# The last quarter of an output, added and stored in two halves of rows

## The chip, the cores and the metric

One core of one Trainium2 chip. The metric is device time in microseconds (us) of the whole program, as a median of runs; the profile's span is some 1.8 us shorter than the time of the same run.

## The reference

```
h   = x @ w1                     # x: 8 x 1024 x 1024, w1: 1024 x 4096
h   = 0.5 * h * (1 + tanh(sqrt(2 / pi) * (h + 0.044715 * h ** 3)))
out = (h @ w2).astype(float32)   # w2: 4096 x 1024, out: 8 x 1024 x 1024 in float32
```

## The kernel before

Both products are made with Strassen-like schemes on blocks; a second level of the scheme ("inner") makes each block product of the second matmul out of seven smaller ones. For the last block of 1024 rows, the last of the seven outer products (number 3) yields four quarters of a 512x512 block of the output. Each quarter is 256 rows by 256 columns: one PSUM bank of 128 partitions with two halves `i` of 256 columns each, where half `i` holds 128 rows of the output.

```python
    def store_quarter(sb, o, b, src):              # one quarter: 2 x 128 rows x 256 columns, 256 KB
        ...
        rows = out2[r0:r0 + HT // 2, o0:o0 + OH // 2].rearrange("(i p) n -> p i n", p=P)
        return nc.sync.dma_start(out=rows, in_=src)

        def multiply(self, j, bank, first):        # 16 matmuls: eight into each half of the bank
            t = self.x[S_TERM[j]] if j in S_TERM else self.s[j]
            for i in range(2):
                for c in range(NI // 2):
                    ...matmul(bank[:, i * OH // 2:(i + 1) * OH // 2], lhsT=t[:, c, i * P:(i + 1) * P], ...)

        def steps(self, into):
            a, b, c = psum(), psum(), psum()
            for n, (j, bank, first, out, adds) in enumerate((
                (1, a, True, "11", ()),
                ...                                # 2, 6, 5, 7
                (3, b, True, None, ("12",)),
                (4, a, False, "21", ()),           # the last step: adds onto bank a, gives quarter 21
            ), 1):
                self.multiply(j, bank, first)
                if out is not None:
                    t = quarter(into, out)
                    ...
                        tt(t, quarter(self.base, out), pair(bank), ADD, True)    # one VectorE add, 128x512
                ...
                        self.part(o, quarter(into, o))                           # the store of a quarter
                yield n

        # in matmul2, for the last block of rows:
        products[7].rows = out("22", accum_op=ADD)     # two 512 KB stores that add into the output
        if end:
            products[3].part = lambda b, t: store_quarter(sb, "12", b, t)
```

All semaphores and waits are placed by the program builder from the order of these calls. Transfers over SyncE's queue and over GpSimd's queue each use eight semaphores in rotation.

## Time and profile before

| | kernel before |
|---|---|
| time, median of the first three runs | 1487.91 us (1487.71 to 1488.25) |
| span of the profiled run | 1486.0 us |
| last matmul ends at | 1482.15 us |
| last add | 1482.26 to 1482.95 us |
| last store issued, landed | 1482.98, 1485.10 us |

The page and the timeline are shown in the prediction. One more view answers to a view of the changed kernel later: who SyncE waited for in the last four microseconds (engine and line, what it waited for: total us, times, longest).

```profile
SPq L1064 <- DMA out_dram<-u: 1.3, 2, 0.9
```

Line 1064 is the close of the program. Two of its waits lasted: one until the third quarter's store had landed, and one of 0.9 us until the last had. A wait that finds its store landed takes a few hundredths of a microsecond and is not in this list.

### The profile page before, as it was taken

To read this page: it belongs to the slowest core of one execution; us is meant where nothing else is said; L and a number is where in the kernel's file an instruction comes from. 1 tells how busy PE (TensorE), PEld (TensorE's weight loads), DVE (VectorE), ACT (ScalarE), POOL (GpSimd) and SP (SyncE) were. 2 spreads that over 40 slices of the span, in tenths; PEclk is the share of its full clock that TensorE was granted. 3 is DMA by queue.
4 is the path that set the end of the run, shared out by engine and by line. 5 is a ranking of instruction groups with operands and counts; after the bars stand their busy time and mean duration, and the time that the engine had idled before them with its cause. 6 is when DMAs were issued, how large, how long until landed. Compare 5 with 4: busy or idle time off the path is not lost.

```text
span 1486.0 us, 26324 instructions
## 1 busy us (share of the span) xinstructions
PE 1477.3 (99%) x9879; PEld 964.2 (65%) x9879; DVE 1149.5 (77%) x1792; ACT 613.3 (41%) x1154; POOL 231.8 (16%) x311
## 2 busy tenths in 40 slices
PE   9999999999999999999999999999999999999998
PEld 5444444444455787558875588655886568855687
DVE  6657458767677898779987799877997779877887
ACT  5665026621166412663136621366214652056510
POOL 2542222222211012100022001210111101101011
PEclk9999999999999999999999999999999999999999
DMA  9999798987997999989999899998999989997886
GB/s 331 340 355 404 202 363 291 405 269 228 383 288 173 358 306 308 336 203 386 303 307 340 222 364 307 311 305 244 353 305 321 307 263 340 294 373 240 297 279 212
DMA packets 242719, 453.70 MB, mean 305 GB/s; under 512 B 80672, under 2 KB 85792, under 8 KB 241696
## 3 DMA queue, kind: packets, MB, share of 16 engines
q1 hardware_dynamic: 215680, 358.69, 71.6%
q0 software_dynamic: 26912, 93.34, 21.3%
q8 instruction: 77, 1.26, 0.3%
q14 instruction: 50, 0.41, 0.1%
HBM read 355.47 MB, written 111.15 MB: 314 GB/s over the span
## 4 chain that ended last, share of the span: by engine, by line
PE 97%; DVE 1%; DMA 1%; issue 0%; ACT 0%; DVEq 0%
PE ps L438 49%; PE ps L902 35%; PE ps L943 13%; PE ps L368 1%; DVE tmp L119 1%; DMA out_dram<-tmp 0%; PE ps L345 0%; DMA u<-in_x_dram 0%; DVE u L119 0%; ACT u L135 0%; ACT tmp L135 0%; PE ps L303 0%; DVE tmp L337 0%; DVE u L356 0%; DVEq L119 0%
## 5 line engine op out<-in xcount | busy, mean ns | idle before, releaser
L438 PE MATMUL ps<-u 128*128 128x512 f16 (+1 forms) x4104 | 746.7, 344 | 2.3 <-DVE tmp L119 2.3
L119 DVE TENSOR_TENSOR tmp<-tmp,ps 128x256 f32<-128x256 f32 (+1 forms) x930 | 450.7, 532 | 273.9 <-PE ps L438 169.4
L438 PEld LDWEIGHTS <-u 128*128 128x128 f16 x4104 | 401.1, 98 | 345.3 <-issue 11.0
L135 ACT COPY tmp<-ps 128x512 f32<-128x512 f32 x410 | 231.3, 581 | 302.1 <-PE ps L438 154.1
L451 ACT ACTIVATE g<-tmp 128x512 f16<-128x512 f32 x378 | 238.1, 633 | 165.2 <-DVE tmp L119 165.0
L902 PE MATMUL ps<-u,gc 128*128 128x256 f16 x2688 | 300.4, 273 | 0.0
L902 PEld LDWEIGHTS <-gc 128*128 128x128 f16 x2688 | 262.5, 98 | 31.2
L902 PE MATMUL ps<-u,g 128*128 128x256 f16 x2016 | 227.9, 273 | 0.0
L119 DVE TENSOR_TENSOR u<-u 128x2048 f16<-128x2048 f16 (+3 forms) x292 | 219.5, 790 | 9.2 <-DMA raw_d<-u 2.5
L135 ACT COPY u<-ps 128x512 f32<-128x512 f32 (+1 forms) x134 | 77.9, 587 | 348.9 <-PE ps L902 341.4
L902 PEld LDWEIGHTS <-g 128*128 128x128 f16 x2016 | 197.3, 98 | 24.1
L689 POOL DMA_DIRECT2D out_dram<-u x70 | 64.0, 989 | 710.5 <-issue 366.0
L119 DVE TENSOR_TENSOR u<-u,ps 128x512 f32<-128x512 f32 x216 | 147.7, 684 | 34.7 <-PE ps L902 28.5
L943 PE MATMUL ps<-u,g 128*128 128x512 f16 x768 | 166.4, 379 | 0.0
L943 PEld LDWEIGHTS <-g 128*128 128x128 f16 x768 | 75.1, 98 | 90.6
L119 DVE TENSOR_TENSOR g<-g,g 128x2048 f16<-128x2048 f16 (+1 forms) x136 | 130.3, 980 | 1.6 <-ACT g L451 1.6
L119 DVE TENSOR_TENSOR gc<-g,gc 128x2048 f16<-128x2048 f16 x84 | 102.4, 1219 | 0.6
L119 DVE TENSOR_TENSOR gc<-g 128x2048 f16<-128x2048 f16 x78 | 95.0, 1218 | 0.0
L451 ACT ACTIVATE g<-ps 128x512 f16<-128x512 f32 x134 | 79.9, 597 | 13.9 <-PE ps L438 6.9
L138 POOL CAST u<-gc 128x1024 f16<-128x1024 f32 x40 | 47.2, 1190 | 64.7 <-DMA gc<-in_w_dram 61.7
L415 POOL COPY pace<-g 128x2 f16<-128x2 f16 x24 | 4.4, 185 | 191.4 <-ACT g L451 191.4
L536 POOL TENSOR_TENSOR gc<-g 128x2048 f16<-128x2048 f16 x6 | 24.4, 4063 | 62.1 <-ACT g L451 62.1
(37 smaller groups left out, 257.3 us busy)
## 6 DMA issues: line engine op xcount, KB each, us to landing
u<-w_d SPq DMA_DIRECT2D x336, 256.0 KB, 6.5
u<-in_d SPq DMA_DIRECT2D x168, 512.0 KB, 7.1
u<-raw_d SPq DMA_DIRECT2D x252, 256.0 KB, 7.1
out_dram<-u POOLq DMA_DIRECT2D x70, 512.0 KB, 9.3
gc<-in_w_dram SPq DMA_DIRECT2D x48, 512.0 KB, 6.3
u<-in_d SPq DMA_DIRECT2D x96, 256.0 KB, 7.4
raw_d<-u SPq DMA_DIRECT2D x32, 512.0 KB, 8.9
u<-raw_d SPq DMA_DIRECT2D x32, 512.0 KB, 14.1
```

The costliest lines, as they stand in the source:

```text
L119: i = nc.vector.tensor_tensor(out=out, in0=in0, in1=in1, op=op)
L135: tc.keep_in_program_order(nc.scalar.copy(out=out, in_=in_))
L138: pool_last[0] = nc.gpsimd.tensor_copy(out=out, in_=in_)
L368: tc.keep_in_program_order(nc.tensor.matmul(bank[:, cols], lhsT=w[:, k, :], rhs=self.xs.blocks[f"{a}{r}"][:, k, cols], start=r == 1 and k ...
L415: mark = nc.gpsimd.tensor_copy(out=pace, in_=g_chunk[:, :2])
L438: tc.keep_in_program_order(nc.tensor.matmul(bank, lhsT=w, rhs=x, start=first and k == 0, stop=k == n - 1, skip_group_check=not first,))
L451: gelu_last[0] = nc.scalar.activation(out=g[b][:, c, :], in_=src, func=GELU)
L536: nc.gpsimd.tensor_tensor(out=early[7], in0=u, in1=v, op=SUB)
L689: return nc.gpsimd.dma_start(out=rows, in_=src, **kw)
L902: tc.keep_in_program_order(nc.tensor.matmul(bank[:, i * OH // 2:(i + 1) * OH // 2], lhsT=t[:, c, i * P:(i + 1) * P], rhs=self.y[j][:, c, : ...
L943: tc.keep_in_program_order(nc.tensor.matmul(pair(bank), lhsT=a[:, c, :], rhs=chunks(pieces[c // QC])[:, :, c % QC, :], start=(first and c ...
```

## The change

The intent is to shorten the tail behind the last matmul: the last quarter is added in two halves, so that the first half's store can start while the second is added, and the second store is issued by ScalarE, which need not wait for SyncE.

```diff
+    def store_eighth(sb, o, b, i, src):
+        r0 = sb * SB + (int(o[0]) - 1) * HT + (int(b[0]) - 1) * HT // 2 + i * P
+        o0 = (int(o[1]) - 1) * OH + (int(b[1]) - 1) * OH // 2
+        dma = (nc.sync, nc.scalar)[i].dma_start
+        return dma(out=out2[r0:r0 + P, o0:o0 + OH // 2], in_=src)
 ...
                 self.multiply(j, bank, first)
+                if self.last is not None and j == 4:
+                    for i in range(2):
+                        t = quarter(into, out)[:, i]
+                        tt(t, quarter(self.base, out)[:, i], pair(bank)[:, i], ADD, True)
+                        self.last(out, i, t)
+                    yield n
+                    return
 ...
         if end:
             products[3].part = lambda b, t: store_quarter(sb, "12", b, t)
+            products[3].last = lambda b, i, t: store_eighth(sb, "12", b, i, t)
```

(The constructor sets `self.last` to `None`.)

More of the change, by code (lines that the diff above doesn't have):

```diff
@@ L871, in __init__ @@
         def __init__(self, m, t, rows=lambda a, t: None, part=lambda b, t: None, base=None):
-            self.m, self.rows, self.part, self.base = m, rows, part, base
+            self.m, self.rows, self.part, self.base, self.last = m, rows, part, base, None
             self.x, self.s, self.y = {b: inner_block(t, b) for b in BLOCKS}, {}, {}
```

## The prediction

> **What bounds the kernel now.** I read the page first: the busy rows and the slices, then the chain that ended last, to see how much of the time the change can touch at all.
>
> ```profile
> span 1486.0 us, 26324 instructions
> PE 1477.3 (99%) x9879; PEld 964.2 (65%) x9879; DVE 1149.5 (77%) x1792; ACT 613.3 (41%) x1154; POOL 231.8 (16%) x311
> ...
> PEclk9999999999999999999999999999999999999999
> ...
> PE 97%; DVE 1%; DMA 1%; issue 0%; ACT 0%; DVEq 0%
> ```
>
> TensorE is the bound: 97% of the chain, busy in every slice, at an undiminished clock (1.00 in the windows below). The change adds or removes no matmul. It touches only the last quarter of the last product, so only what comes after the last matmul can move. That is next: the timeline of the last six microseconds (start, duration, engine, operation, idle before and releaser).
>
> ```profile
> 1480.13 3.21 SPq L683 DMA_DIRECT2D out_dram<-u  x3
> 1480.14 1.74 PEld L902 LDWEIGHTS <-g 128*128 128x128 f16 x16
> 1480.24 1.91 PE L902 MATMUL ps<-u,g 128*128 128x256 f16 x16
> 1480.44 0.69 DVE L119 TENSOR_TENSOR u<-u,ps 128x512 f32<-128x512 f32 x1 [0.34 <-PE ps L902]
> 1482.26 0.69 DVE L119 TENSOR_TENSOR u<-u,ps 128x512 f32<-128x512 f32 x1 [1.13 <-PE ps L902]
> ```
>
> The last 16 matmuls end at 1480.24 + 1.91 = 1482.15. VectorE adds the bank to the base from 1482.26 to 1482.95. The last of the three stores in the merged row is then issued at 1482.98. Its transfer, from the DMA view of 1482 to 1486 (40 slices of 0.1 us), and the table of windows (PE, PEld, DVE, ACT, POOL busy, then clock, DMA share, GB/s):
>
> ```profile
> DMA  9999999999764111002899999940000000000000
> ...
> out_dram<-u SPq DMA_DIRECT2D x1, 256.0 KB, 2.1
> ```
>
> ```profile
> 1482.95:1483.85 0.90, 0.00 (x0) 0.00 (x0) 0.00 (x0) 0.00 (x0) 0.00 (x0) 1.00 0.32 110
> 1483.85:1484.75 0.90, 0.00 (x0) 0.00 (x0) 0.00 (x0) 0.00 (x0) 0.00 (x0) 1.00 0.87 291
> 1484.75:1485.15 0.40, 0.00 (x0) 0.00 (x0) 0.00 (x0) 0.00 (x0) 0.00 (x0) 1.00 0.00 0
> ```
>
> The engines are busy with the third quarter until about 1483.3, nearly idle to 1483.8, full from 1483.9 to 1484.7, then still. So the last 256 KB cost 0.87 us from issue to the first packet (1482.98 to 1483.85), 0.87 us of packets (to 1484.72) and 0.38 us to the last semaphore update (1485.10): together the 2.1 us to landing that the row gives. From the landing to the end of the span, 0.90 us remain. They are the closing waits and the all-engine barrier. The single records at the closing line show SyncE taking nine closing waits one after another; the first seven have nothing to wait for and follow each other every 0.062 us (1483.40 to 1483.76), the eighth passes at 1484.16 when the third quarter has landed, the ninth at 1485.12 when the last has. The barrier then takes 1485.19 to 1486.01 = 0.82 us.
>
> The whole stretch behind the last matmul is thus 1486.01 - 1482.15 = 3.86 us, or 0.26% of the span. Even if all of it vanished, the verdict would not leave 2%.
>
> **What the Trainium skill says.** "DMA: Bandwidth & Descriptors", section "Issuing engines are not separate DMA queues", says that DMAs from different issuing engines run on the same 16 DMA engines and that a second issuer saves only the sequencer's issue time. Here one issue on SyncE takes 0.37 us, so that is what the second queue can save. No ScalarE issue is in this trace to compare. The same page, "Anatomy of one DMA — SWDGE (gpsimd) path", splits a transfer into a fixed part of about 2 us and a part that grows with bytes. The trace agrees in kind for this other path: 0.87 + 0.38 = 1.25 us are fixed, 0.87 us scale. "VectorE: DVE Perf Modes", section "The TRN2 errata — SBUF-src ops pay a fixed extra latency per instruction", says that a short instruction pays a fixed cost. By form, the adds into `tmp` from PSUM take 417 ns at 128x256 and 683 ns at 128x512, so 2 x 417 - 683 = 151 ns are fixed. "PSUM — Partial Sum Buffer", section "PSUM bank collisions raise a hardware error", says that two engines may not be in one bank at once; I use it in step 1.
>
> **The change part by part.** Removed: one add of 128x512 (0.69 us) and one 256 KB store by SyncE. Added: two adds of 128x256, and two stores of 128 KB, the first by SyncE, the second by ScalarE, idle since 1470.8. Both halves still lie in one PSUM bank, filled by eight matmuls each (0.109 us apart).
>
> Step 1, when the first half may start. Its eight matmuls are done near 1481.28, which would be 0.87 us before the others. But the first half's add would then read a bank into which TensorE is still writing. The records of before show how the program treats that. In the inner products of the first matmul, where the product being drained and the next one lie in different banks, the drained one's last matmul carries a semaphore signal of its own (seen at 1340.41); where the next one fills the other half of the same bank, only that next one's last matmul signals (1340.84, 1346.51). So the whole bank is awaited. I choose: the first half starts at 1482.26, as now.
>
> Step 2, the adds. In the timeline at 1340 a back-to-back pair of such adds takes 0.75 us for both:
>
> ```profile
> 1340.79 0.75 DVE L119 TENSOR_TENSOR tmp<-tmp,ps 128x256 f32<-128x256 f32 x2 [0.95 <-PE ps L438]
> ```
>
> First half 1482.26 to 1482.68, second 1482.59 to 1483.01: +0.06 us for the second against now.
>
> Step 3, the transfers. First half: issue at 1482.71, first packet at 1483.58 (0.87 later). Second half: ScalarE issues at 1483.04, independently of SyncE, first packet at 1483.91 if ScalarE is as quick. 256 KB take 0.87 us in all, so the engines work from 1483.58 to 1484.45 without a gap. Last packet 1484.45, landing at 1484.83 (+0.38), against 1485.10: -0.27 us. A slower ScalarE issue, which no record shows, would eat into that; I allow 0.1 us.
>
> Step 4, the closing waits. The stores by SyncE use eight semaphores in rotation; the last four use the fifth to the eighth. One store more takes the rotation back to the first. The closing waits, in the order of the records, take these eight in the same sequence, one each in the second to ninth wait. Now the latest landing is in the ninth wait. In the changed kernel the second half's semaphore would be in the second, and seven waits would remain after the landing: 7 x 0.062 = 0.43 us that today lie hidden ahead of it. I think this more likely than not, as the rotation looks like one for all hardware-queue stores.
>
> Sum: +0.43 - 0.27 + 0.1 (allowance) = +0.26 us with step 4, -0.17 us without. Weighted by 65 to 35, near +0.1 us; I take no change at all: **1487.9 us**.
>
> **The rivals.** First, the early half: if the first half waits only for its own eight matmuls, its add runs at 1481.39 to 1481.81 beside the other eight, its store leaves at 1481.84 (SyncE is free of the third quarter's issue at 1481.53), and only 128 KB remain at the end. The second half's add would be 1482.26 to 1482.68, issue 1482.71, packets 1483.58 to 1484.02, landing 1484.40: -0.70 us, with step 4 -0.27. The signals at 1340 and 1346 speak against it; 10%. Second, the intended gain alone: the halves overlap as in step 3 and the closing order does not matter, -0.2 to -0.3 us. For it: the closing order could be by age, which this trace cannot tell from the rotation, for both rise together; about a third. Third, a slow second queue: a first use of ScalarE's queue costs 0.3 us or more, which with step 4 makes +0.5 to +0.8. ScalarE's queue is not used in the kernel before, so nothing speaks for or against; 15%. Fourth, contention: a transfer hidden anyway. The third quarter's packets are out by about 1483.3, ahead of 1483.58, so I expect none.
>
> **How the range and the chances follow.** The outcomes span -0.7 to +0.8 us. The three runs of before lie within 1487.71 to 1488.25, so 0.5 us of scatter comes on top. That gives 1486.9 to 1488.8. Being off by 2% would take 30 us, eight times the whole stretch behind the last matmul: 99% within 2%, and half a per cent on either side for something unforeseen in the build.
>
> **What would show each step right or wrong.** Step 1: a timeline in which the first 128x256 add starts about 0.1 us after the last matmul; a start 0.8 us ahead of it would be the first rival. Step 2: two last adds that span 0.75 us. Step 3: two 128 KB stores issued about 0.33 us apart, one under ScalarE's queue, packets without a gap, and the last landing some 0.27 us earlier after the last matmul; a ScalarE issue row much over 0.37 us, or a gap before its packets, would be the third rival. Step 4: from the last landing to the end of the span 1.3 us in place of 0.90. The stretch from the last matmul to the end should be 3.7 to 4.1 us. I would be wrong altogether if the rest of the program were ordered otherwise by the change, so that TensorE's busy time left 1477 us.

## The result, and the profile after

| | before | after |
|---|---|---|
| time, median (range) of 6 runs each | 1488.15 us (1487.71 to 1488.64) | 1488.47 us (1487.75 to 1489.17) |
| ratio | | 1.0002, 95% interval 0.9989 to 1.0015 |
| span of the profiled run | 1486.01 us | 1487.32 us |
| last matmul ends at | 1482.15 us | 1483.15 us |
| last landing, after the last matmul | 2.95 us | 2.83 us |
| from there to the end | 0.90 us | 1.35 us |
| whole stretch behind the last matmul | 3.86 us | 4.17 us |

A ratio is the mean time of one kernel's fast runs over that of the other's of the same rounds, so it is not quite the ratio of the medians.

The timeline of the changed kernel's end (start, duration, engine, operation, idle before and releaser):

```profile
1481.24 1.91 PE L908 MATMUL ps<-u,g 128*128 128x256 f16 x16
...
1483.26 0.75 DVE L119 TENSOR_TENSOR u<-u,ps 128x256 f32<-128x256 f32 x2 [1.13 <-PE ps L908]
1483.70 0.34 SPq L689 DMA_DIRECT2D out_dram<-u  x1
1484.04 0.37 ACTq L689 DMA_DIRECT2D out_dram<-u  x1
```

Both adds come after all 16 matmuls, and the pair takes 0.75 us where the one add took 0.69. The two issues are 0.34 us apart. The DMA view of 1483 to 1487 (40 slices of 0.1 us, then issues with size and median us to landing):

```profile
DMA  8999999999942112999999950000000000000000
...
out_dram<-u SPq DMA_DIRECT2D x1, 128.0 KB, 2.0
out_dram<-u ACTq DMA_DIRECT2D x1, 128.0 KB, 1.9
```

Beside the same view of before, the last packets stand nearer to the earlier ones: the idle gap is four slices long, not five or six. Now SyncE's waits at the end:

```profile
SPq L1078 <- DMA out_dram<-u: 1.8, 1, 1.8
```

There is one long wait at the close (now line 1078) where there were two. It is the wait for ScalarE's store, which stands third in a row of ten closing waits, and in the single records it passes at 1485.99 and seven more follow it, at 1486.06, 1486.12, 1486.18, 1486.24, 1486.30, 1486.36 and 1486.42, some 0.06 us apart. All that these seven wait for had landed; they simply come after. Before, the wait for the last store was the last of nine.

The 1.0 us by which the last matmul stands later is not made at the end. In the single records the lead of before is 1.01 us at the 600th matmul (119 us) and 0.99 us at the last. It arises in the first 48 us, while the first inputs are loaded. The tables of windows, first the kernel before, then the changed one (columns: length, then PE, PEld, DVE, ACT, POOL busy with counts, clock, DMA share, GB/s):

```profile
0.00:48.00 48.00, 45.41 (x272) 25.04 (x273) 31.60 (x42) 28.61 (x50) 12.53 (x16) 1.00 0.98 344
```

```profile
0.00:48.00 48.00, 43.31 (x267) 23.20 (x268) 32.45 (x42) 28.49 (x50) 11.65 (x15) 1.00 0.97 340
```

In 48 us the run of before had started 272 matmuls, the other 267, of the same order of matmuls. The two kernels are the same up to their ends, and the repeats below show that identical kernels differ here too.

### The profile page after: what moved, and what is told of

It reads as the page before. It is cut to its first block, busy times and chain, and to the rows that moved or that the text cites. A ratio compares the mean times of both kernels' runs of the same rounds, so it can differ in the third digit from the quotient of the medians.

```text
span 1487.3 us, 26328 instructions
## 1 busy us (share of the span) xinstructions
PE 1476.2 (99%) x9879; PEld 962.9 (65%) x9879; DVE 1151.7 (77%) x1793; ACT 614.1 (41%) x1154; POOL 227.3 (15%) x311
## 4 chain that ended last, share of the span: by engine, by line
PE 97%; DVE 2%; DMA 1%; issue 0%; ACT 0%; SPq 0%; DVEq 0%
PE ps L438 48%; PE ps L908 35%; PE ps L956 13%; DVE tmp L119 1%; PE ps L368 1%; DMA gc<-in_w_dram 1%; DVE u L119 1%; SPq L132 0%; DVE g L119 0%; PE ps L345 0%; ACT tmp L135 0%; ACT u L196 0%; DVE u L196 0%; ACT g L451 0%; DVE u L356 0%
## 5 line engine op out<-in xcount | busy, mean ns | idle before, releaser
L119 DVE TENSOR_TENSOR u<-u,ps 128x512 f32<-128x512 f32 (+1 forms) x217 | 147.8, 682 | 34.7 <-PE ps L908 28.5
```

The source lines that it names most:

```text
L119: i = nc.vector.tensor_tensor(out=out, in0=in0, in1=in1, op=op)
```

## The experiments

Twelve runs; all but the last four give a correct result. A store's semaphore gets 16 updates in these traces, which I read as one from each of the 16 DMA engines. The lag of a store is the time of its last update less that of its third last; the table's times count from the end of the last matmul, in us, out of single records of the trace.

| run | last matmul | lag of the third quarter's store | third last update of the last store | its last update | from there to the end | whole stretch |
|---|---|---|---|---|---|---|
| before | 1482.15 | 0.45 | 2.91 | 2.95 | 0.90 | 3.86 |
| before_again | 1482.58 | 0.62 | 2.91 | 2.96 | 0.90 | 3.86 |
| after | 1483.15 | 0.63 | 2.62 | 2.83 | 1.35 | 4.17 |
| after_again | 1482.37 | 0.77 | 2.62 | 3.14 | 1.33 | 4.47 |
| both_sync | 1482.56 | 1.08 | 2.74 | 3.38 | 1.34 | 4.72 |
| before_early_sem | 1483.09 | 0.16 | 2.92 | 2.95 | 1.34 | 4.29 |
| after_late_sem | 1483.89 | 0.16 | 2.62 | 2.65 | 0.90 | 3.55 |
| late_sem_again | 1482.14 | 0.53 | 2.63 | 2.74 | 0.92 | 3.65 |
| two_banks | 1483.36 | 0.48 | 2.49 | 2.82 | 1.33 | 4.15 |
| two_banks_late | 1482.17 | 0.58 | 2.35 | 2.94 | 0.91 | 3.85 |
| after_plain | 1482.56 | 0.06 | 2.61 | 2.65 | 1.34 | 3.99 |
| after_plain_2 | 1482.52 | 0.05 | 2.61 | 2.64 | 1.34 | 3.99 |
| after_none | 1482.74 | 0.04 | 2.61 | 2.66 | 1.34 | 4.01 |
| two_banks_late_plain | 1482.68 | 0.05 | 2.19 | 2.23 | 0.92 | 3.15 |

My theory was that the halves do land earlier, and that the place of the second half's semaphore in the row of closing waits gives more than that back (the closing order). The main rival was that the second queue itself costs.

**The changed kernel again.** No edit.

> The changed kernel unaltered, for a second profile beside which the others of this call are read. In the first profile the stretch from the last matmul to the end was 4.17 us (2.83 us to the last landing, then 1.35 us), against 3.86 us before (2.95 and 0.90). Theory of the closing order: the part after the last landing is set by how many closing waits follow the one for the last store, so it repeats at 1.33 to 1.37 us; the part to the landing may move by 0.2 us with the last semaphore update of one DMA engine. If the 1.35 us were scatter of the run, it would not repeat. The start (the last matmul stood 1.0 us later than in the profile of before, and all of that arose within the first 160 us) should move from run to run. Time against before: within 0.5 us, not to be told apart.

Measured: 1488.64 us (1488.13 to 1489.43, 5 runs) against 1487.95 us for before (1487.60 to 1488.37, 9 runs), ratio 1.0005 (0.9992 to 1.0018). The part behind the landing repeated (1.33 us). The landing moved by 0.31 us, more than the 0.2 us that I allowed; only the last DMA engines did so, for the third last update is at 2.62 us in both profiles. The start was a run of its own: the last matmul stood 0.78 us earlier than in the first profile of the same kernel.

**Both halves over SyncE.**

```diff
-        dma = (nc.sync, nc.scalar)[i].dma_start
+        dma = nc.sync.dma_start
```

> Both halves are stored over SyncE's queue, ScalarE's is not used. Theory of the closing order: the second store still gets the first semaphore of the rotation, so the part from the last landing to the end stays near 1.35 us (perhaps 0.06 less, as ScalarE's own state need not be waited for); the second issue starts when SyncE is free of the first, 0.35 us after it, where ScalarE started 0.335 us after it, so the landing is the same within 0.1 us. Rival, the second queue is what costs: the part after the landing falls to the 0.90 us of before, or the landing comes at least 0.2 us earlier.

Measured: 1488.34 us (1488.03 to 1489.06, 5 runs), ratio 1.0002 (0.9989 to 1.0016). Its waits of SyncE at the end:

```profile
SPq L1078 <- DMA out_dram<-u: 1.9, 1, 1.9
```

Again there is one long wait, and 1.34 us behind the landing, without any use of ScalarE's queue. The second queue is not what costs. My guess of 0.06 us less was wrong. What ScalarE's queue saves can be read as well: SyncE issued the second half 0.99 us after the last matmul, ScalarE 0.89 us, and the third last update came at 2.74 against 2.62 us. That is 0.1 us. The last landing, 3.38 us, missed the 0.1 us that I expected; it is a poor measure here, as this run had the largest lag of all.

**The changed kernel with the second half's semaphore last.** The first quarter's store, issued some 7 us before the last matmul ends, goes over GpSimd's queue. Then one store fewer is in the rotation.

```diff
-        return nc.sync.dma_start(out=rows, in_=src)
+        return (nc.gpsimd if b == "11" else nc.sync).dma_start(out=rows, in_=src)
```

> The changed kernel, but the first quarter's store goes over GpSimd's queue, so that one hardware-queue store fewer is made and the second half's store gets the last semaphore of the rotation. Theory of the closing order: its wait is the last of the closing waits, and the part from the last landing to the end falls from 1.35 to about 0.90 us; with the landing at 2.7 to 2.85 us after the last matmul the whole stretch is 3.6 to 3.75 us, 0.1 to 0.25 us under before. Rival, the second queue or the barrier costs: the part after the landing stays at 1.35 us.

Measured: 1488.91 us (1487.56 to 1489.37, 5 runs), ratio 1.0004 (0.9992 to 1.0017). The waits:

```profile
SPq L1078 <- DMA out_dram<-u: 1.2, 3, 0.5
```

There are three shorter waits now, the last of them for the last store, with nothing behind it. From the landing to the end it takes 0.90 us, as before the change, with ScalarE's queue in use. The whole stretch is 3.55 us, 0.31 us under before.

**The kernel before with its last semaphore first.** The converse: the last quarter is left whole, and the first quarter is stored in two halves, which moves the rotation on by one.

```diff
-            products[3].part = lambda b, t: store_quarter(sb, "12", b, t)
+            products[3].part = lambda b, t: (
+                [store_eighth(sb, "12", b, i, t[:, i]) for i in range(2)]     # both over SyncE
+                if b == "11" else store_quarter(sb, "12", b, t)
+            )
```

> The kernel before, but its first quarter is stored in two halves, both over SyncE, long before the end; the last quarter is added and stored whole as before. This only moves the last store's semaphore to the first of the rotation. Theory of the closing order: the landing stays at 2.95 us after the last matmul, and the part after it grows from 0.90 to about 1.3 us, so the whole stretch is 4.25 to 4.35 us, longer than in the changed kernel. Rival, the second queue or the halving of the last quarter is what makes the end long: 0.90 us and 3.86 us as before.

Measured: 1489.16 us (1488.20 to 1490.26, 5 runs), ratio 1.0008 (0.9995 to 1.0020). Timeline and waits of its end:

```profile
1483.19 0.69 DVE L119 TENSOR_TENSOR u<-u,ps 128x512 f32<-128x512 f32 x1 [1.13 <-PE ps L908]
1483.91 0.37 SPq L683 DMA_DIRECT2D out_dram<-u  x1
```

```profile
SPq L1073 <- DMA out_dram<-u: 1.7, 1, 1.7
```

The add and the store are those of before, and so is the landing at 2.95 us; but the close takes 1.34 us in place of 0.90. This and the run before it settle the closing order: the same 0.43 us come and go with the place of one semaphore, with and without the change.

**The kernel before again.** No edit.

> The kernel before, unaltered, for a second profile and to see what two identical kernels show in these rounds. Closing-order theory: the part after the last landing is 0.90 us again. Open beside it: one of the 16 DMA engines finished the changed kernel's last store later than the others in three profiles (last semaphore update 0.2 to 0.6 us after the third last), in the profile of before by 0.04 us only. If this backlog is scatter of the earlier stores, the store of the third quarter here shows a lag anywhere between 0.1 and 1.1 us, and the last store less of it, as the engines are nearly idle for 0.5 us ahead of it; landing 2.95 to 3.3 us after the last matmul. The last matmul should stand anywhere between 1482 and 1484 us, decided in the first 50 us.

Measured: 1488.18 us (1487.86 to 1488.22, 5 runs) against the 1488.02 us of the reference runs (1487.71 to 1489.07, 9 runs), ratio 0.9999 (0.9986 to 1.0011). The stretch is 3.86 us again, although the third quarter's store lagged by 0.62 us here. The last store lags by 0.05 us only. I read this as the whole quarter leaving late enough for the lagging engine to have caught up; no run tests this alone.

**The late semaphore again.**

> The changed kernel with the second half's store on the last semaphore of the rotation, for a second profile. Closing-order theory: 0.90 us after the last landing again. The landing is 2.65 us after the last matmul if no DMA engine lags, as in the first profile, and up to 3.2 us if one lags as in the other profiles; if the lag stays away again, making one store fewer on this queue may be what takes it away.

Measured: 1487.62 us (1487.51 to 1488.69, 5 runs), ratio 0.9997 (0.9983 to 1.0011). Behind the landing 0.92 us, stretch 3.65 us. The lag was back (0.53 us in the third quarter's store), so making one store fewer is not what takes it away.

**Two banks for the last step.** The second half's eight matmuls go to a bank of their own; what the accumulating bank already held for that half is added to the base some steps earlier.

```diff
                 if self.last is not None and j == 4:
+                    other = psum()
+                    self.multiply(j, bank, first, other)       # half 1 starts afresh in `other`
                     for i in range(2):
                         t = quarter(into, out)[:, i]
-                        tt(t, quarter(self.base, out)[:, i], pair(bank)[:, i], ADD, True)
+                        if i == 0:
+                            tt(t, quarter(self.base, out)[:, i], pair(bank)[:, i], ADD, True)
+                        else:
+                            tt(t, t, other[:, :OH // 2], ADD, True)
                         self.last(out, i, t)
 ...
+                if self.last is not None and j == 7:
+                    t = quarter(into, "21")[:, 1]
+                    tt(t, quarter(self.base, "21")[:, 1], pair(bank)[:, 1], ADD, True)
```

> The changed kernel, but the last step writes its two halves into two PSUM banks: the first half goes on in the accumulating bank, the second starts in a bank of its own, and the accumulated part of the second half is added to the base some steps earlier. Theory that the whole bank is awaited: the first half's add now starts near 0.77 us before the end of the last matmul in place of 0.11 us after it, its store is issued near 0.3 us before it, and the second half's landing comes at 2.4 to 2.5 us after the last matmul (the engines are then busy without a gap: third quarter to 1.2, first half to 1.6, second half to 2.0, plus 0.38) where the changed kernel has 2.65 without a lagging engine. The semaphore order is that of the changed kernel, so 1.34 us follow: 3.75 us in all. Rival, that a whole step's signal and not the bank is awaited: the add stays at 0.11 us after the last matmul and nothing is gained.

Measured: 1488.02 us (1487.73 to 1489.29, 4 runs), ratio 1.0000 (0.9986 to 1.0013). Its timeline, where the last matmul ends at 1483.36:

```profile
1482.60 0.42 DVE L119 TENSOR_TENSOR u<-u,ps 128x256 f32<-128x256 f32 x1 [0.26 <-PE ps L909]
1483.04 0.34 SPq L689 DMA_DIRECT2D out_dram<-u  x1
1483.40 0.42 DVE L119 TENSOR_TENSOR u<-u,ps 128x256 f32<-128x256 f32 x1 [0.38 <-PE ps L909]
1483.85 0.37 ACTq L689 DMA_DIRECT2D out_dram<-u  x1
```

The first add starts 0.76 us ahead of the last matmul's end, and its store leaves at 1483.04. So it was the shared bank (or the buffer that fills it; the two are one here) that held the first half back. The landing was a miss: 2.82 us, not 2.4 to 2.5. The third last update is at 2.49 us. Here more than one engine was behind: of the 16 updates of the third quarter's store nine came by 1.39 us after the last matmul, and seven from 1.61 to 2.30 us.

**Both repairs.**

> Both repairs together: two banks for the last step and the second half's store on the last semaphore. If both theories hold the parts add: landing at 2.4 to 2.5 us, then 0.90 us, 3.3 to 3.4 us in all, some 0.5 us under before and 0.8 us under the changed kernel. In the measured time that is 0.03 to 0.05% and may stay below the scatter of the start.

Measured: 1487.84 us (1487.36 to 1488.43, 5 runs), ratio 0.9997 (0.9985 to 1.0010). The stretch was 3.85 us, no better than before. The close was as expected (0.91 us), the landing was not: 2.94 us, with the third last update at 2.35 us. The parts of the gain are there on most engines, and a lag of 0.59 us takes it all.

**What makes an engine lag.** In the last 25 us of these traces the lag is first seen at two 512 KB stores of GpSimd, issued some 11 us before the last matmul ends, which add into the output. The edit replaces the addition by a plain write; the last kernel of the group leaves the two stores out.

```diff
-        products[7].rows = out("22", accum_op=ADD)
+        products[7].rows = out("22") if end else out("22", accum_op=ADD)
```

> Wrong result on purpose. The changed kernel, but the two 512 KB stores of the seventh product near the end write plainly, where they accumulate into the output as it is. So far one DMA engine landed its share of the third quarter's store 0.16 to 1.08 us after the third last engine, and of the changed kernel's last store 0.2 to 0.6 us; the lag is first seen at the landing of these accumulating stores, 5 us before the last matmul, and is under 0.05 us in the stores of 15 us before it. Theory that the accumulating stores leave a backlog on one engine: third quarter's lag and last store's lag fall below 0.15 us, the landing comes at 2.62 us after the last matmul, and 1.34 us follow: 3.96 us. Rival, the bytes near the end or the engine itself: the lag stays at 0.2 us or more.

> Wrong result on purpose. The same kernel as the one before it in this call once more, since the lag is scattered: if the accumulating stores make it, it stays below 0.15 us here too; if it does not in one of the two, the theory falls.

> Wrong result on purpose. The changed kernel without the two accumulating stores at all. Theory of the backlog by these stores: lag below 0.15 us and landing at 2.62 us, as with plain stores. If plain stores keep the lag and this takes it away, it is their bytes; if this keeps it too, it comes from the later stores or the engine. After the landing 1.34 us in every case.

> Wrong result on purpose. Two banks, last semaphore and plain stores in place of accumulating ones. With accumulating stores it landed at 2.94 us where 2.36 us held for the third last engine. Theory of the backlog: landing at 2.3 to 2.45 us, then 0.90 us, 3.2 to 3.35 us in all, the shortest stretch of all. Rival: a lag of 0.2 us or more stays and the stretch is 3.5 us or more.

Measured, one run each (so their state is unknown, and their times of 1488.35, 1488.28, 1488.53 and 1487.60 us decide nothing; all four give a wrong result): the lag is at most 0.06 us in the third quarter's store in all four, and the last store's landing is within 0.05 us of its third last update. The two stores of the seventh product, in the changed kernel, and then with plain writes (issues, and us from issue to landing):

```profile
L695 POOL DMA_DIRECT2D out_dram<-u x2: 1227/1468/1710, 1471.7 to 1472.5; - x2
...
DMA to landing us min/median/max: 6.5/7.5/8.5
```

```profile
L695 POOL DMA_DIRECT2D out_dram<-u x2: 727/727/727, 1471.1 to 1471.8; - x2
...
DMA to landing us min/median/max: 3.2/3.6/4.0
```

The accumulating stores take twice as long to land (7.5 against 3.6 us in the median) and leave behind them one or more engines that are late for the stores that follow closely. All four runs were on one chip, on which no unaltered kernel was profiled, but the chip is not the reason: in the trace of after_plain two earlier accumulating stores, which the edit left as they were, lag by 0.28 and 1.08 us (issued at 1433.8 and 1434.6 us). Nor do only accumulating stores lag: in the same trace a plain store at 1422.4 us, with loads keeping the DMA engines busy, lags by 1.65 us. What is shown is that near this end, with no loads left, the two accumulating stores make the lag. With plain writes the second repair shows its worth: two_banks_late_plain has its landing at 2.23 us, better than the 2.3 to 2.45 expected, and the shortest stretch of all, 3.15 us. Whether the adding itself delays an engine, or the longer occupation of all of them, is open, as is which engine it is.

No correct version stands out in the measured time. The late semaphore gave 3.55 and 3.65 us behind the last matmul against 3.86 us before, 0.2 to 0.3 us in 1488; its two medians, 1488.91 and 1487.62 us, differ from each other by far more.

## Why the prediction was right or wrong

The outcome was inside the range, but that proves little: the range was built to take in every outcome considered, from -0.7 to +0.8 us, and the scatter on top. The steps are judged by the traces. Three of the four held, and the third held in part.

- **The bound.** Right. With the start-up's scatter aside, nothing moved ahead of the last matmul: from the start of the 260th (45 to 47 us) to the end of the last it takes 1436.75 to 1436.78 us in all fourteen profiles. Its sign of failure, a changed busy time of TensorE, did appear in a small way (1476.2 in place of 1477.3 us), but in the first 48 us, where the repeats scatter as well, and without a changed order of matmuls.
- **Step 1, the bank.** Right: the first add starts 0.11 us after the last matmul. The two-bank kernel shows the cause.
- **Step 2, the adds.** Right: 0.75 us for the pair.
- **Step 3, the transfers.** Right for most of the engines and wrong for the last. ScalarE issued as quickly as SyncE (0.37 us), so the 0.1 us of allowance was not needed and the third rival is out. The 0.37 us of a whole issue that I put down as what the second queue can save was too much: the second half's add ends only 0.30 us after the first issue starts, and the saving was 0.1 us (both_sync). The third last update came 0.29 us earlier, 2.62 against 2.91 us, where 0.27 us was worked out. But a store has landed when its last engine is done, and that came 0.12 us earlier in one profile and 0.19 us later in the other (2.95 us before; 2.83 and 3.14 us after). The statement that failed is in the fourth rival, "The third quarter's packets are out by about 1483.3, ahead of 1483.58, so I expect none." I took the DMA view's mean of 16 engines for each of them: the low digits behind 1483.3 were two engines still at work, whose updates for the third quarter came at 1.87 and 1.99 us after the last matmul, when the other 14 had sent theirs by 1.54 us. Before the change they had caught up when the last store came, and an earlier store meets them.
- **Step 4, the closing waits.** Right in mechanism and size: 1.3 us foretold, 1.33 to 1.35 measured, against 0.90. One detail was off: there are ten closing waits, not nine, and the store's is the third; seven follow it, as foretold.
- **The sum.** With step 4 and the allowance it was +0.26 us; the two profiles of the changed kernel gave +0.31 and +0.61 us behind the last matmul, and with plain stores, where no engine lagged, it was +0.13 us (3.99 against 3.86), near the +0.16 us of steps 3 and 4 without the allowance. I weighted it down to no change. The median rose by 0.32 us, which the scatter of the runs does not let one call real.
- **The scatter.** Mis-sized: I put 0.5 us on top, from three runs. The changed kernel's runs span 1.4 us, and a variant of the kernel before 2.1 us. Where a run was profiled, the scatter of the last matmul's place is made in the first 48 us.

## What to carry to other kernels

Ask of the last store not only when it lands but what the program does between the landing and its end: here the place of one semaphore in the closing row was worth 0.43 us, more than the halving was. A transfer ends with its slowest engine, so look at the last updates of its semaphore, not at the mean DMA share, before an idle gap ahead of it is taken for waste. Here two halves that shared a PSUM bank were read only when both were written, and with a bank of its own the first half's add started 0.87 us earlier against the last matmul; what that gains depends on the queue of transfers behind it.

## What the Trainium skill lacked or had wrong

- No page has the cost of the closing waits' order. A closing wait that finds its store landed takes 0.06 us; seven of them behind the last landing make 0.43 us (1.33 to 1.35 us from landing to end in the eight profiles with the last store's semaphore early in the row, 0.90 to 0.92 us in the six with it last).
- "DMA: Bandwidth & Descriptors", section "Issuing engines are not separate DMA queues", says that a second issuing engine saves only the sequencer's issue time. The runs agree, and put a number to it that the page lacks: 0.1 us for the second of two 128 KB stores (issue 0.89 against 0.99 us after the last matmul).
- The same page, section "Latency and other measured facts", gives about 600 ns to the first byte for this path. In the single records it was 0.84 to 0.89 us here from the start of the issue to the first packet, and 0.50 to 0.52 us from the issue's end, so the page's figure should say from where it counts.
- The same page, section "Rules for kernel authors", sends accumulating DMAs over GpSimd's queue, without a price. Two such stores of 512 KB landed after 6.5 and 8.5 us in the changed kernel, plain ones after 3.2 and 4.0 us. The third quarter's store, issued some 10 us later, had a lag of 0.16 to 1.08 us in the ten profiles with them, and of 0.04 to 0.06 us in the four without.
